# A hybrid diffusion backbone on one core: two conditioning groups move from VectorE reductions to TensorE matmuls

## The chip, the core and the metric

The kernel runs on one core of a Trainium2 chip. TensorE (PE) multiplies, VectorE (DVE), ScalarE (ACT) and GpSimd (POOL) do everything else, and SyncE (SP) issues most of the DMAs. Each engine runs its own list of instructions strictly in order and waits where an operand is not there yet. The metric is the device time of one execution in microseconds. The kernel before has a median of 2817.92 us over three runs (2812.58 to 2819.59).

## What is computed

The program is two layers over 1024 latent tokens and 256 context tokens of width 1024. The first layer mixes with a Fourier transform and a long convolution, the second with attention. What matters here is the conditioning. Each layer turns the two conditioning vectors `c` and `c_ctx` into six groups of 1024 modulation values each:

```python
def ada_mod(cond, w, b):
    m = (jax.nn.silu(cond) @ w + b)[..., None, :]
    return jnp.split(m, 6, axis=-1)

sh1, sc1, g1, sh2, sc2, g2 = ada_mod(c, ada_w[i], ada_b[i])
u_lat = modulate(rms_norm(h_lat, norm1_g[i]), sh1, sc1)
...
h_lat = h_lat + g1 * y_lat
h_lat = h_lat + g2 * swiglu(modulate(rms_norm(h_lat, norm2_g[i]), sh2, sc2), ...)
```

The first two groups of layer 0 (`sh1`, `sc1`) are needed at the very start. The third and fourth (`g1`, the gate behind the mixer, and `sh2`, the shift ahead of the feed-forward part) are needed only when the output projection of the mixer is evicted, several hundred microseconds later. All of it is 32-bit arithmetic.

## The kernel before, in words

Activations lie with channels on the 128 partitions. A modulation value is therefore a column: `self.ada[(layer, c)]` is a tile of 128 x 48, and column `nb` holds outputs 128·nb to 128·nb+127. A group is eight such columns, and two groups are sixteen blocks of 128 outputs.

The program is written as Python generators that are stepped in turn. `in_proj` (L1091) walks over sixteen blocks of the input projection. For each block it loads one 128 x 1024 slice of `w_in`, splits it into a high and a low part on ACT and DVE, and multiplies. Between the matmuls of a block it steps filler generators: the filters of the long convolution (`long` and `filt`), the small Fourier part, and `ada`. The table of numbers at its call (L2833 and L2834) says how many steps of each filler belong to which block; `ada` begins with the sixth block. A planner then sets the final order on each engine from its own estimate of when things are ready, so that the lists of PE, DVE, ACT, POOL and SP that run on the chip are fixed before the run.

`ada_first` (L501) makes the first two groups on TensorE. The two vectors stand as 2 columns, the weights move past them 512 outputs at a time, and the 2 x 512 result is a row. Tiny matmuls of 2 x 128 against an identity (L348, from the helper `mm`) turn the row into columns, and DVE adds the bias.

`late_groups((2, 3), "ws")` (L621) makes the third and fourth group on VectorE. `load_cond` (L539) brings `c` and `c_ctx` to all 128 partitions and applies Silu on ACT. `ada_group` (L550) loads one 512 KB block of `ada_w` ahead of its use, into a tile of the ring `ws`, which has four buffers and also serves the loads of `w_in`. `ada_block` (L572) then makes four multiply-and-sum reductions over 512 elements (L580): two halves for each of the two vectors. The lines that follow use these names: L580 is the reduction, L333 the DMA from SP's queue, L844 the product of a filter with its window, L352 and L354 the high and the low part of a split, L1085 to L1088 the short convolution.

Of the kernel before, what the change touches and what calls it, by code (L numbers as in the profile page):

```python
# [16 lines left out]
MUL, ADD, SUB, MAX, MIN = ALU.mult, ALU.add, ALU.subtract, ALU.max, ALU.min  # L17

P = 128
D = 1024  # L20
KB = D // P
# [14 lines left out]
def _f32(a):  # L36
    return np.ascontiguousarray(a, dtype=np.float32)
# [221 lines left out]
class Builder:  # L259
# [241 lines left out]
    def ada_first(self):  # L501

        nc, a = self.nc, self.a
        cond = self.C(16)
        self.ld(cond, a["cond"])
        nc.scalar.activation(cond, cond, AF.Silu)
        yield

        def columns(m, ps):
            col = self.PS()  # L510
            for j in (0, 1):
                row = self.G()
                nc.vector.tensor_copy(row[0:2, :], ps[j][0:2, :])
                for k in range(4):
                    nb = 4 * j + k
                    with self.follow(last):
                        self.mm(col[:, 2 * nb:2 * nb + 2], row[0:2, k * P:(k + 1) * P], self.ident[0:2, 0:2], True, True)
            sl = slice(m * 8, m * 8 + 8)
            for c in (0, 1):
                t = self.ada[(0, c)]  # L520
                nc.vector.tensor_tensor(t[:, sl], col[:, 0:16].rearrange("p (n c) -> p c n", c=2)[:, c],
                                        self.adab[:, sl], ADD)
                if m == 1:
                    nc.vector.scalar_tensor_tensor(t[:, sl], t[:, sl], 1.0, self.gs[:, 0:8], op0=ADD, op1=MUL)

        ps = {}
        for m in (1, 0):
            ps[m] = [self.PP(), self.PP()]
            for kb in range(KB):
                w = self.W("ws", "ws") if m == 0 and kb > KB - 3 else self.S4()  # L530
                self.ldr(w, a["ada_k"][m, kb])
                for j in (0, 1):
                    last = nc.tensor.matmul(ps[m][j][0:2, :], cond[:, 2 * kb:2 * kb + 2], w[:, j * 512:(j + 1) * 512],
                                            start=kb == 0, stop=kb == KB - 1).ins
                yield
        for m in (1, 0):
            columns(m, ps[m])
# [55 lines left out]
    def ada_stream(self, groups, n):  # L593

        blocks = [(l, m, m * 8 + k, conds) for l, m, conds in groups for k in range(8)]

        def step(b, st):
            l, m, nb, conds = b
            self.ada_block(l, nb, [st[:, :512], st[:, 512:]], conds)
            if nb % 8 == 7:  # L600
                self.ada_done(l, m, conds)

        own = [self.S4() for _ in range(3)]
        for k in range(0, n, 3):
            with self.follow(self.last_hi):
                for t, b in zip(own, blocks[k:k + 3]):
                    self.lda(t, self.a["ada_w"][b[0], b[2]])
            yield
            with self.follow(self.last_lo):
                for t, b in zip(own, blocks[k:k + 3]):  # L610
                    step(b, t)
            yield
        for k, b in enumerate(blocks[n:]):
            t = own[k % 3]
            with self.follow(self.last_ldr):
                self.ldr(t, self.a["ada_w"][b[0], b[2]])
            with self.follow(self.last_lo):
                step(b, t)
            yield

    def late_groups(self, ms, where):  # L621

        self.load_cond(wide=where == "s4")
        for m in ms:
            yield from self.ada_group(0, m, (0, 1), where)
# [2144 lines left out]
    def run(self):  # L2770
        nc, a = self.nc, self.a
# [27 lines left out]
        def filters():  # L2799
            gens = [self.filter_raw("l", raws["l"], (o,)) for o in (0, 1)]  # L2800
            next(gens[0])
            yield
            for o in (0, 1):
                tot = self.filter_sum("l", o, raws["l"][o])
                for k, _ in enumerate(gens[o]):
                    if k > 1 and k % 2 == 0:
                        next(tot)
                    yield
                for k, _ in enumerate(self.spectrum_l(o, raws["l"][o], tot)):
                    if o == 0 and k == 5:  # L2810
                        next(gens[1])
                    yield

        long = filters()
        ada = self.late_groups((2, 3), "ws")
        filt = (x for o in (0, 1) for g in (self.filter_raw("c", raws["c"], (o,)), self.spectrum_c(o, raws["c"][o]))
                for x in g)
        self.Y = {}
# [2 lines left out]
        def four():  # L2821
            y.t.update(self.new_act(pcs=(2,), blocks=range(4)).t)
            yield from self.fourier_c(y)

        def conv():
# [5 lines left out]

        fc, cc = four(), conv()
        self.in_proj(u, ng, ((long, (1, 2, 4, 5, 5, 5, 5, 5, 6, 0)), (filt, (0,) * 9 + (3, 3, 3, 3, 2)),  # L2833
                             (ada, (0,) * 5 + (1, 1, 2, 1, 2, 1, 2, 1, 2, 1, 2))), fc, cc)  # L2834
        self.held = False
        for i in range(8):
            self.tap(f"u{i}", u.ap(0, i, 0))
# [120 lines left out]
        h2, o, h4 = Act(), Act(), Act()  # L2958
# [62 lines left out]
        for i, _ in enumerate(first_part(1)):  # L3021
            if i == 7:
                c = self.rms_begin(0)
# [53 lines left out]
        c = self.rms_begin(1)  # L3077
# [11 lines left out]
def host_layout(i):  # L3089
    f = {k: np.asarray(v) for k, v in i.items()}  # L3090
    o = {}
    o["x_t"] = f["x"][0].T.reshape(KB, P, LAT)
    o["ctx_t"] = f["ctx"][0].T.reshape(4, 2, P, CTX).transpose(0, 2, 1, 3).reshape(4, P, 512)
    o["x_row"] = np.concatenate([f["x"][0], f["ctx"][0]]).reshape(10, P, D)
    o["c"] = f["c"].reshape(1, D)
    o["c_ctx"] = f["c_ctx"].reshape(1, D)
    o["ada_k"] = f["ada_w"][0, :, :2 * D].reshape(KB, P, 2, D).transpose(2, 0, 1, 3)
    o["cond"] = np.stack([f["c"].reshape(KB, P), f["c_ctx"].reshape(KB, P)], axis=1).transpose(2, 0, 1).reshape(P, 16)
    o["ada_w"] = f["ada_w"].transpose(0, 2, 1).reshape(2, 48, P, D)
    o["ada_b"] = f["ada_b"].reshape(96, P).T  # L3100
    gs = np.concatenate([f["norm1_g"].reshape(16, P), f["norm2_g"].reshape(16, P), f["final_g"].reshape(8, P)])
    o["gs"] = gs.T

    def wblk(w):
        k, n = w.shape
        return w.reshape(k // P, P, n // P, P).transpose(2, 1, 0, 3).reshape(n // P, P, k)

    o["w_in"] = wblk(f["ab_w_in"][0])
    o["w_out"] = wblk(f["ab_w_out"][0])
    o["w_out2"] = wblk(f["na_w_out"][0])  # L3110
    o["gate"] = np.stack([wblk(f["ffn_w_gate"][l]) for l in range(2)])
    o["up"] = np.stack([wblk(f["ffn_w_up"][l]) for l in range(2)])
    o["down"] = f["ffn_w_down"].reshape(2, NFB, P, 2, 512).transpose(0, 1, 3, 2, 4)
    qkv = f["na_w_qkv"][0]
    o["wq"] = wblk(qkv[:, :D])
    o["wk"] = wblk(qkv[:, D:2 * D])
    o["wv"] = qkv[:, 2 * D:].reshape(4, 2, P, 2, 512).transpose(3, 0, 2, 1, 4).reshape(2, 4, P, 1024)
    w1, w2 = f["hy_f_w1"][0], f["hy_f_w2"][0]
    z1 = np.zeros((66, P), np.float32)
    z1[:33, :64], z1[33:, 64:] = w1, w1  # L3120
    z2 = np.zeros((P, P), np.float32)
    z2[:64, :64], z2[64:, 64:] = w2, w2
    o["w1f"], o["w2f"] = z1, z2
    o["mlpv"] = np.stack([np.tile(f[k][0], 2) for k in ("hy_f_b1", "hy_f_b2", "hy_f_freq")], axis=1)
    o["w3"] = np.concatenate([f["hy_f_w3"][0]] * 2, axis=0)
    cw = np.concatenate([f["hy_conv_w"][0], f["hy_conv_b"]], axis=0)
    o["conv"] = cw.reshape(4, 12, P).transpose(2, 0, 1).reshape(P, 48)
    o["skip"] = f["hy_bias"][0].reshape(8, P).T
    o["skiprow"] = f["hy_bias"][0].reshape(2, HC)
    rpb = f["na_rpb"][0]  # L3130
    bias = np.full((16, 2, 4, P, 384), NEG, np.float32)
    for hf in range(2):
        for r in range(8):
            row = 8 * hf + r
            rs = min(max(row - 4, 0), 8)
            for c in range(4):
                for w in range(16):
                    qc = 16 * c + w
                    ws = min(max(qc - 8, 0), 48)
                    for kr in range(rs, rs + 8):  # L3140
                        c0 = (kr - 4 * hf) * 32 + ws - KSTART[c]
                        dc = ws - qc + 15
                        bias[:, hf, c, r * 16 + w, c0:c0 + 16] = rpb[:, kr - row + 7, dc:dc + 16]
    o["bias"] = bias
    return {k: _f32(v) for k, v in o.items()}
# [20 lines left out]
```

## Time and profile before

| | |
|---|---|
| median of three runs | 2817.92 us (2812.58 to 2819.59) |
| the profiled execution's own time | 2812.72 us |
| its span, first to last instruction | 2810.8 us |
| PE busy | 2695.3 us, 96% of the span |
| DVE busy | 2129.7 us, 76% |
| ACT busy | 1631.0 us, 58% |
| mean granted TensorE clock | 0.986 |
| sixteen blocks of the two groups: loads issued | from 104.4 us to 433.7 us |
| their reductions on DVE | from 240.2 us to about 457 us |

The columns of the views are these. A row of the stretches gives the busy time of PE, PE's weight load, DVE, ACT and POOL with the number of instructions in brackets, then the granted TensorE clock as a share of full speed, the DMA share and the rate in GB/s. A row of the groups gives line, engine, operation, output and inputs by tile name, shapes and count, and after the bar the busy time, the mean length of one in ns, and the idle time of the engine just before with what ended it. A row of the waits gives who waited, for whom, the total in us, the number of times and the longest. A row of the timeline gives the start in us, the length in us, and in square brackets the idle time ahead of it with what ended it. Matmuls are pipelined: the length of one is longer than the distance to the next, so a price per matmul is read from start to start.

### The profile page before, as it was taken

The numbers are of one execution on the slowest core, as the hardware profiler recorded it, in microseconds if no ns is written. First come the engines' busy times: TensorE is split into PE (matmuls) and PEld (weight loads), VectorE is DVE, ScalarE is ACT, GpSimd is POOL, SyncE is SP. The second block draws the span as 40 slices with busy tenths as digits, with TensorE's granted clock in tenths as the row PEclk, the third lists the DMA queues.
The fourth block names the chain that finished last, engine by engine and source line by source line (L and its number), as shares of the span: only waits on it lengthen the run. The fifth ranks groups of instructions, "written<-read, shape, count | busy, mean of one in ns | idle before, by whom it ended". The sixth has DMA issues, their size and how long they took to land. (4 is left out here: it accounts for less than half of the span.)

```text
span 2810.8 us, 44489 instructions
## 1 busy us (share of the span) xinstructions
PE 2695.3 (96%) x15570; PEld 1717.7 (61%) x15570; DVE 2129.7 (76%) x3870; ACT 1631.0 (58%) x3005; POOL 514.1 (18%) x820
## 2 busy tenths in 40 slices
PE   6999889999999999999999999999989999999998
PEld 3877677878889444444446646767677544444445
DVE  4678788868776899987798646878786877775775
ACT  3533324543487666767556736888774655654653
POOL 2120233351101011122011002333222012221000
PEclk9999899999999999999999999999999999999999
DMA  7244736766655787787988746788955246654863
GB/s 267 95 148 164 226 93 196 232 197 226 213 168 173 244 292 287 284 314 276 360 308 287 238 153 161 193 202 199 253 180 192 89 140 222 224 191 168 296 224 105
DMA packets 312317, 595.92 MB, mean 212 GB/s; under 512 B 83352, under 2 KB 130138, under 8 KB 312094
## 3 DMA queue, kind: packets, MB, share of 16 engines
q1 hardware_dynamic: 241374, 378.61, 42.6%
q0 software_dynamic: 53760, 158.38, 16.3%
q10 hardware_dynamic: 16960, 56.11, 5.8%
q8 instruction: 122, 2.00, 0.3%
q14 instruction: 101, 0.83, 0.1%
HBM read 445.64 MB, written 119.80 MB: 201 GB/s over the span
## 5 line engine op out<-in xcount | busy, mean ns | idle before, releaser
L2080 PE MATMUL ps<-s,s 128*128 128x512 f16 x2280 | 508.9, 379 | 5.6 <-DVE s L2104 3.1
L2080 PEld LDWEIGHTS <-s 128*128 128x128 f16 x2640 | 258.0, 98 | 320.5 <-issue 10.1
L348 PE MATMUL ps<-s,wh 128*128 128x256 f32 (+1 forms) x1784 | 413.8, 334 | 9.3 <-ACT wh L352 6.1
L348 PEld LDWEIGHTS ps<-s,wh 128*128 128x128 f32 x1784 | 300.3, 191 | 44.6 <-ACT wh L352 8.0
L2344 PE MATMUL ps<-s 128*128 128x512 f16 (+2 forms) x1404 | 316.1, 376 | 0.2 <-ACT s L2334 0.2
L2344 PEld LDWEIGHTS <-s 128*128 128x128 f16 x1716 | 166.1, 98 | 196.1 <-issue 5.3
L348 PE MATMUL ps<-s,wl 128*128 128x256 f32 (+1 forms) x892 | 273.0, 332 | 3.2 <-DVE wl L354 3.2
L2334 ACT ACTIVATE s<-s,c 128x512 f16<-128x512 f32 (+1 forms) x300 | 199.9, 714 | 118.7 <-DMA s<-d 63.0
L348 PE MATMUL ps<-s,s 128*128 128x65 f16 (+4 forms) x2748 | 242.4, 238 | 19.3 <-DMA s<-tk 5.0
L2335 DVE SCALAR_TENSOR_TENSOR s<-s,c,s 128x512 f16<-128x512 f32 (+1 forms) x300 | 208.6, 747 | 33.2 <-ACT s L2334 32.7
L339 POOL DMA_DIRECT2D d<-s x245 | 132.9, 544 | 503.6 <-DVE s L2197 170.5
L2080 PE MATMUL ps<-s,hl 128*128 128x512 f16 x924 | 212.2, 379 | 1.2 <-ACT hl L1933 1.2
L348 PE MATMUL pq<-s,hl 128*128 128x512 f16 (+1 forms) x960 | 206.9, 358 | 0.4 <-DVE s L2587 0.4
L348 PEld LDWEIGHTS ps<-s,wl 128*128 128x128 f32 x892 | 168.2, 192 | 21.9 <-DVE wl L354 4.9
L2080 PEld LDWEIGHTS <-hl 128*128 128x128 f16 x1056 | 103.2, 98 | 125.9 <-ACT hl L1933 1.4
L1933 ACT ACTIVATE hl<-ws,c 128x1024 f16<-128x1024 f32 x89 | 101.8, 1144 | 107.8 <-DMA ws<-in_up 37.7
L1934 DVE SCALAR_TENSOR_TENSOR hl<-ws,c,hl 128x1024 f16<-128x1024 f32 x89 | 114.0, 1283 | 62.6 <-ACT hl L1933 62.3
L348 PEld LDWEIGHTS <-s 128*128 128x128 f16 x2400 | 115.2, 98 | 66.8 <-DMA s<-tk 5.7
L348 PEld LDWEIGHTS ps<-s,s 128*128 128x128 f32 (+1 forms) x828 | 128.6, 191 | 35.7 <-PE ps L348 9.5
L1934 DVE SCALAR_TENSOR_TENSOR s<-t,c,s 128x512 f16<-128x512 f32 x176 | 126.6, 747 | 26.3 <-ACT s L1933 26.3
L348 PEld LDWEIGHTS <-hl 128*128 128x128 f16 x960 | 86.8, 98 | 80.3 <-issue 8.8
L1933 ACT ACTIVATE s<-t,c 128x512 f16<-128x512 f32 x176 | 118.1, 714 | 9.2 <-DVE t L2059 5.6
(541 smaller groups left out, 5115.9 us busy)
## 6 DMA issues: line engine op xcount, KB each, us to landing
s<-d SPq DMA_DIRECT2D x326, 256.0 KB, 4.9
d<-s POOLq DMA_DIRECT2D x229, 256.0 KB, 4.5
s<-in_down SPq DMA_DIRECT2D x150, 256.0 KB, 6.4
ws<-in_gate SPq DMA_DIRECT2D x42, 512.0 KB, 4.7
ws<-in_up SPq DMA_DIRECT2D x42, 512.0 KB, 6.0
s<-in_ada_w POOLq DMA_DIRECT2D x34, 512.0 KB, 6.5
d<-s SPq DMA_DIRECT2D x60, 256.0 KB, 2.5
s<-in_ada_w ACTq DMA_DIRECT2D x30, 512.0 KB, 7.4
```

What stands on the lines that cost most here:

```text
L339: self.last_ldr = self.nc.gpsimd.dma_start(out, in_).ins
L348: self.last_mm = self.nc.tensor.matmul(o, l, r, start=st, stop=sp).ins
L1933: self.last_hi = self.nc.scalar.activation(hi, src, AF.Copy, scale=s).ins
L1934: self.last_lo = self.nc.vector.scalar_tensor_tensor(lo, src, s, hi, op0=MUL, op1=SUB).ins
L2080: nc.tensor.matmul(ps, x[:, sl], y, start=first and j == 0 and x is wh and y is xh, stop=j == 3 and x is wl, skip_group_check=True)
L2334: self.last_hi = nc.scalar.activation(x, f[:, c:c + 512], AF.Copy, scale=s).ins
L2335: self.last_lo = nc.vector.scalar_tensor_tensor(y, f[:, c:c + 512], s, self.raw_part(x), op0=MUL, op1=SUB).ins
L2344: m = nc.tensor.matmul(acc[j][:, c0:c1], x[:, sl], y[:, xs], start=first and k == 0, stop=last and k == 2, skip_group_check=True)
```

## The change

The third and fourth group go to TensorE. Sixteen slices of the weights are laid out on the host as blocks of 128 outputs, with the 1024 inputs as eight slabs of 128 (`ada_c`). For each block, eight matmuls of 128 moving columns run against the two conditioning columns that `ada_first` already made (`condc`), and their sum is a row pair of 2 x 128 in a PSUM tile of the `ps` ring. DVE copies the 2 x 128 row pair into the front of the block's own weight tile. One step of the generator later, a tiny matmul against the identity turns the pair into two columns in the same PSUM tile, and two DVE additions of 128 x 1 put them into `self.ada` with the bias. The broadcast loads of `c` and `c_ctx` for these groups and their Silu go away. The load stays 512 KB a block, one block ahead, in the same ring, but a tile of the ring is now free after the turn rather than after the last reduction. The last entries of the step table go from `1, 2` to `2, 2`, since the last turn needs one more step. The later groups keep their reductions on DVE.

```diff
-        cond = self.C(16)
+        cond = self.condc = self.C(16)
...
+    def column_groups(self, ms):
+
+        nc, a = self.nc, self.a
+        blocks = [m * 8 + k for m in ms for k in range(8)]
+        ready = []
+
+        def load(nb):
+            t = self.W("ws", "ws")
+            self.ld(t, a["ada_c"][nb - 16])
+            ready.append(t)
+
+        load(blocks[0])
+        for k, nb in enumerate(blocks):
+            if k + 1 < len(blocks):
+                load(blocks[k + 1])
+            w = ready.pop(0)
+            ps = self.PP()
+            for kb in range(KB):
+                self.mm(ps[0:2, 0:P], self.condc[:, 2 * kb:2 * kb + 2], w[:, kb * P:kb * P + P], kb == 0, kb == KB - 1)
+            nc.vector.tensor_copy(w[0:2, 0:P], ps[0:2, 0:P])
+            yield
+            self.mm(ps[:, P:P + 2], w[0:2, 0:P], self.ident[0:2, 0:2], True, True)
+            for c in (0, 1):
+                nc.vector.tensor_tensor(self.ada[(0, c)][:, nb:nb + 1], ps[:, P + c:P + c + 1], self.adab[:, nb:nb + 1],
+                                        ADD)
...
-        ada = self.late_groups((2, 3), "ws")
+        ada = self.column_groups((2, 3))
...
-                             (ada, (0,) * 5 + (1, 1, 2, 1, 2, 1, 2, 1, 2, 1, 2))), fc, cc)
+                             (ada, (0,) * 5 + (1, 1, 2, 1, 2, 1, 2, 1, 2, 2, 2))), fc, cc)
...
+    o["ada_c"] = f["ada_w"][0, :, 2 * D:4 * D].reshape(KB, P, 16, P).transpose(2, 1, 0, 3).reshape(16, P, D)
```

The first place is on PE, in the filters of the context tokens inside the input projection. `s_48` holds their hidden values, `g` a scaled filter weight, `pq` and `ps` are PSUM tiles. Before:

```order
L348 MATMUL pq_3016<-g_2994,s_48_172 128x512
L348 MATMUL pq_3070<-s_783_2882,s_798_2912 128x256
L348 MATMUL pq_3070<-s_783_2882,s_799_2913 128x256
L348 MATMUL pq_3070<-s_783_2882,s_798_2912 128x256
L348 MATMUL ps_3082<-s_783_2882,s_798_2912 128x256
L348 MATMUL ps_3082<-s_783_2882,s_799_2913 128x256
L348 MATMUL ps_3082<-s_783_2882,s_798_2912 128x256
L348 MATMUL ps_3011<-g_2989,s_48_172 128x512
L348 MATMUL pq_3016<-g_2995,s_48_172 128x512
```

With the change:

```order
L348 MATMUL ps_3045<-ws_2876,c_102 2x128 x8
L348 MATMUL ps_3021<-g_2999,s_48_172 128x512
L348 MATMUL ps_3069<-ws_3043,c_102 2x128
L348 MATMUL pq_3026<-g_3004,s_48_172 128x512
L348 MATMUL ps_3069<-ws_3043,c_102 2x128 x3
L348 MATMUL pq_3026<-g_3005,s_48_172 128x512
L348 MATMUL ps_3069<-ws_3043,c_102 2x128 x4
L348 MATMUL pq_3090<-s_764_2892,s_779_2922 128x256
L348 MATMUL pq_3090<-s_764_2892,s_780_2923 128x256
L348 MATMUL pq_3090<-s_764_2892,s_779_2922 128x256
L348 MATMUL ps_3045<-c_86,ws_2876 128x2
```

Two blocks' matmuls (`ws` is the weight block, `c_102` the two vectors) now stand among the filter's, and the turn of the first of them (`c_86` is the identity) comes three matmuls after the second block's last one.

The second place is DVE's list around the same filter products. L844 in the kernel before is L870 in the changed one, and L640 and L644 are the copy and the additions of the change. Before:

```order
L580 ISA t_3054,c_98<-ws_3030,s_559_2066,ah_3051 128x512
L580 ISA c_98 128x1
L580 ISA ws_3030,ah_3056<-ws_3030,s_556_2059,c_101 128x512
L580 ISA ah_3056 128x1
L844 TENSOR_TENSOR s_820_3014<-ps_3011,s_817_2998 128x512
L844 TENSOR_TENSOR s_822_3019<-pq_3016,s_817_2998 128x512
```

With the change:

```order
L354 TENSOR_TENSOR g_3005<-t_3002,g_3004 128x512
L640 COPY ws_2876<-ps_3045 2x128
L870 TENSOR_TENSOR s_801_3024<-ps_3021,s_798_3008 128x512
L870 TENSOR_TENSOR s_803_3029<-pq_3026,s_798_3008 128x512
L640 COPY ws_3043<-ps_3069 2x128
L644 TENSOR_TENSOR c_97<-ps_3045,c_101 128x1
L644 TENSOR_TENSOR c_98<-ps_3045,c_101 128x1
```

The reductions ahead of the filter products are gone, and one copy of 2 x 128 stands there. The second copy stands behind both products.

## The prediction

> **What bounds the kernel now.** I read the page first, then stretches of time around the change, then who waits there, then the instructions that the change removes or resembles. The page says that TensorE is busy nearly all the time and that the chain that ended last is made of its matmuls.
>
> ```profile
> span 2810.8 us, 44489 instructions
> PE 2695.3 (96%) x15570; PEld 1717.7 (61%) x15570; DVE 2129.7 (76%) x3870; ACT 1631.0 (58%) x3005; POOL 514.1 (18%) x820
> PE 23%; DVE 2%; ACT 1%; issue 0%; DMA 0%; DVEq 0%; POOL 0%; ACTq 0%
> ```
>
> So time saved on DVE counts only where PE stands still, and every microsecond added to PE counts unless it lands in a hole. The average hides where the holes are; the stretches show it.
>
> ```profile
> core 0: us, PE busy (x) PEld busy (x) DVE busy (x) ACT busy (x) POOL busy (x), PEclk, DMA share, GB/s
> 80.00:160.00 80.00, 79.54 (x435) 68.00 (x434) 55.55 (x108) 36.66 (x71) 16.67 (x22) 1.00 0.33 107
> 160.00:190.00 30.00, 29.21 (x141) 21.82 (x141) 22.27 (x47) 10.94 (x22) 6.45 (x12) 0.94 0.54 167
> 190.00:460.00 270.00, 239.50 (x1134) 190.55 (x1133) 223.81 (x487) 94.06 (x172) 52.22 (x71) 0.93 0.52 162
> 340.00:350.00 10.00, 7.90 (x31) 7.05 (x32) 9.74 (x35) 2.61 (x9) 0.49 (x1) 0.50 0.61 191
> ```
>
> From 190 to 460 us, the rest of the input projection, PE idles 270 - 239.5 = 30.5 us. Its granted clock is 0.93 there, so 7% of the cycles are missing; over the 239.5 busy us that is 16.8 us of work done slowly. At full clock and without holes this stretch holds 239.5 - 16.8 = 222.7 us of PE work, and 47.3 us are slack. DVE is at 223.8 of 270, 83%. In 340 to 350 DVE is full (9.74 of 10), PE has holes, and the clock is at half. From 80 to 160, with DVE at 55.55 of 80 (69%), PE is full at clock 1.00.
>
> The waits of PE in that stretch:
>
> ```profile
> PE ps L348 <- ACT s L352: 10.3, 6, 3.8
> PE ps L348 <- ACT g L352: 6.3, 3, 2.9
> PE ps L348 <- DVE s L354: 3.6, 3, 2.2
> PE ps L348 <- DMA tk<-in_ff_l: 2.2, 1, 2.2
> PE ps L348 <- DVE s L1633: 1.9, 1, 1.9
> PE ps L348 <- DVE s L844: 1.8, 1, 1.8
> ```
>
> These are operands that ACT and DVE split. One of them shows how the conditioning takes part:
>
> ```profile
> 342.82 0.74 DVE L580 CUSTOM_DVE_ANT_0 ws<-ws,s,ah 128x512 f32<-128x512 f32 x1
> 343.49 0.74 DVE L580 CUSTOM_DVE_ANT_0 t<-ws,s,ah 128x512 f32<-128x512 f32 x1
> 344.16 0.74 DVE L580 CUSTOM_DVE_ANT_0 ws<-ws,s,c 128x512 f32<-128x512 f32 x1
> 345.44 0.68 DVE L844 TENSOR_TENSOR s<-pq,s 128x512 f32<-128x512 f32 x1
> 345.57 0.80 PE L348 MATMUL ps<-s,wh 128*128 128x256 f32 x2 [1.82 <-DVE s L844]
> ```
>
> Three reductions stand ahead of a filter product on DVE, and PE waits 1.82 us for it.
>
> **What goes.** The reductions and their accumulator reads:
>
> ```profile
> L580 DVE CUSTOM_DVE_ANT_0 t<-ws,s,c 128x512 f32<-128x512 f32 x16 | 13.3, 831 | 0.4 <-ACT s L547 0.4
> L580 DVE CUSTOM_DVE_ANT_0 ws<-ws,s,ah 128x512 f32<-128x512 f32 x16 | 12.5, 780 | 0.0
> L580 DVE CUSTOM_DVE_ANT_0 ws<-ws,s,c 128x512 f32<-128x512 f32 x16 | 12.3, 770 | 0.0
> L580 DVE CUSTOM_DVE_ANT_0 t<-ws,s,ah 128x512 f32<-128x512 f32 x16 | 12.3, 769 | 0.0
> 190.00:460.00 270.00, 48.99 (x128) 0.93 0.52 162
> ```
>
> The last row is the same stretch for L580 alone: 49.0 us of DVE time (the four groups sum to 50.4, since neighbours overlap a little at their ends). Four Silu on ACT and four broadcast loads on SP go too; a table load on ACT moves to the next group's Silu. I cost these at nothing either way, as ACT is busy only 94.1 of 270. If that cover were gone they would be worth a little, all on the gaining side.
>
> **What comes on PE.** 128 matmuls of 128 moving columns and 16 turns. A 32-bit matmul of this kind is recorded as two instructions: the first two groups have 16 x 2 matmuls of 512 columns and 64 records. So 256 and 32 instructions come. Their nearest rows, with the start of what follows each:
>
> ```profile
> 39.56 13.04 PE L533 MATMUL ps<-s,c 128*2 128x512 f32 x30
> 52.43 3.60 PE L533 MATMUL ps<-ws,c 128*2 128x512 f32 x8
> 58.31 1.94 PE L348 MATMUL pq<-c,g 2*128 2x2 f32 x16
> 60.18 0.44 PE L740 MATMUL pq<-c,s 128*128 128x128 f32 x2
> 466.00 1.97 PE L1299 MATMUL ps<-c,s 128*128 128x128 f32 x8 [4.43 <-DVE s L354]
> ```
>
> 512 columns take (52.43 - 39.56)/30 = 0.429 us from start to start, a quarter of that is 0.107. The tiny turns take (60.18 - 58.31)/16 = 0.117, though they move only two columns. No row has 2 stationary and 128 moving columns. The low end is 0.107; the high end is the 0.246 of the last row (1.97/8), 128 columns right after a hole. I take 0.117, because it is measured in dense work and the scaled price lies just below it: 256 x 0.117 = 30.0 and 32 x 0.117 = 3.7, together 33.7 us (31.1 to 66.7).
>
> The Trainium skill, TensorE: Matmul & The Clock Gate, section Back-to-back issue gap, gives about 81 ns for each pair of weight load and matmul at 128 columns in a sustained stream, and FP8 and Floating Point Precision, section TensorE Precision Notes, gives four passes to a true 32-bit matmul. By these an estimate would be 128 x 4 x 0.081 = 41.5 us in place of 30.0. The measured 0.429 us for two passes of 512 speaks for the lower price, and no row here has the case itself.
>
> **What comes on DVE.** Sixteen copies of 2 x 128 and 32 additions of 128 x 1, both out of PSUM:
>
> ```profile
> L513 DVE COPY g<-ps 2x512 f32<-2x512 f32 x4 | 2.7, 679 | 15.4 <-PE ps L533 15.4
> 163.17 0.16 DVE L885 COPY c<-ps 128x4 f32<-128x4 f32 x1
> L1087 DVE SCALAR_TENSOR_TENSOR s<-ps,c,s 128x1 f32<-128x1 f32 x10 | 2.1, 208 | 0.0
> ```
>
> Between 0.16 us for 4 and 0.68 for 512 elements, 128 come to 0.16 + 0.52 x 124/508 = 0.29 us. That is 16 x 0.29 + 32 x 0.208 = 11.3 us. DVE falls to 223.8 - 49.0 + 11.3 = 186.1 us, 69% of 270, the share that it has from 80 to 160.
>
> **The sum.** PE then holds 222.7 + 33.7 = 256.4 us at full clock in a stretch that now takes 270. What is left of the slack decides. From 80 to 160 PE works at 99.4% of its full rate (79.54/80), from 160 to 190 at 91.5% (29.21 x 0.94/30), with DVE at 74%. Neither range has reductions. The stretch in question has filters and spectra like the second and a DVE share like the first, so I take the middle, 95%: 256.4/0.95 = 269.9, no change. The bounds are 256.4/0.994 = 257.9 (-12) and 256.4/0.915 = 280.2 (+10).
>
> The change adds one wait: a turn on PE waits for its copy on DVE, and behind it in PE's list stand the projection's own matmuls, whose results DVE and ACT want next. At the place shown, the turn is three matmuls behind the last of the second block, and its copy has one split ahead of it. Nothing, if the copy has run by then, to some 0.7 us if it stands behind one more 128 x 512 instruction (0.68 us, L844 above); I take 0.25 on average, 16 x 0.25 = +4. The ring brings a wait on the other side: SP waited for the reductions to free its buffers, and the stores behind it waited too.
>
> ```profile
> SPq L333 <- DVE c L580: 37.0, 9, 18.8
> ws<-in_ada_w SPq DMA_DIRECT2D x16, 512.0 KB, 3.7
> ```
>
> Now the turn frees them. A block lands in 3.7 us and is issued a step ahead, sixteen steps in 270 us, so I cost the loads at nothing; if that cover went, each late block would hold PE for up to 3.7 us. Other orders behind 460 us shift by a few instructions; I take zero, a few microseconds both ways.
>
> So the profiled execution of 2812.7 us (span 2810.8 and 1.9 around it) would become 2816.7. The median of the runs lies 5.2 above that execution; carried to it, the forecast is 2817.9 + 4 = 2822 us, a change within 0.3% (8.4 us, about what a measurement of this kernel tells from none).
>
> **The rivals.** First, faster: DVE's relief closes the holes as from 80 to 160, and the filling keeps the clock up. For it, DVE's share becomes the same, and the half clock at 340 to 350 sits beside full DVE. Against it, ACT's splits and one DMA are named in the waits too, and the holes from 160 to 190 come without any reduction. It gives -12, with the turns hidden: 2806 us.
>
> Second, slower: the turns become PE's new wait. PE cannot pass a turn whose copy is behind DVE work, sixteen times. In full stretches a copy stands behind two or three instructions of 0.68 to 0.8 us; at 1.2 us a turn this costs 16 x 1.2 = 19 in place of 4, so 2837 us. Its point: above 0.53 us a turn, 8.4/16, the change is slower by more than 0.3%. For it, DVE is still 69% busy and its list is strict; against it, the planner spread most turns several matmuls behind the copies. The same side is reached if PE only gets the 91.5% of 160 to 190.
>
> Third, slower by the price of the matmuls: the weight load does not hide behind 128 columns as it does behind 512.
>
> ```profile
> L533 PEld LDWEIGHTS ps<-s,c 128*2 128x2 f32 x56 | 4.8, 88 | 30.5 <-issue 17.4 <-DMA s<-in_ada_k 13.0
> ```
>
> Each then costs 0.107 + 0.088 = 0.195 us: 256 x 0.195 + 3.7 = 53.6 us, so (222.7 + 53.6)/0.95 = 290.8, and with the turns +25: 2843 us. Against it, the turns keep 0.117 with a load each. The 81 ns of the skill would come out between, at (222.7 + 41.5 + 3.7)/0.95 = 282 and +16 with the turns.
>
> **How the numbers follow.** The forecast, within 0.3%, has 0.42. Faster has 0.25. The second rival has 0.27 and the third 0.06, together 0.33 for slower. The forecast's own range is 2809 to 2826. The range for 8 in 10 takes in the first rival with a few microseconds below and the second with a few above: 2802 to 2840.
>
> **What would show it.** Right: from 190 to about 465 us PE is above 93% busy at a clock of 0.96 or more, DVE falls to about 69%, the new matmuls stand 0.11 to 0.12 us apart, and PE's waits for the copy sum to under 8 us. The first rival would show the projection ending 10 us earlier. The second would show PE waiting for the copies as its first row of waits. The third would show the new matmuls near 0.2 us apart with PE busy. I would be wrong altogether if the time moved behind 460 us, where only the order of a few loads and matmuls differs.

## The result, and the profile after

The kernel with the change takes 2834.3 us (median of four runs, 2833.45 to 2836.54). The kernel before, on the same chip, takes 2815.9 us (2812.58 to 2819.59). The ratio is 1.0059, with a 95% interval of 1.0044 to 1.0074: slower by 0.6%, 18.4 us. That lies inside the range of 2802 to 2840, but in the case to which the prediction gave 0.33, not in its likeliest.

The page of the profile after, first three parts (busy time, share of the span, instructions; then the chain that ended last, by engine):

```profile
span 2832.0 us, 44960 instructions
PE 2731.8 (96%) x15858; PEld 1737.9 (61%) x15858; DVE 2094.0 (74%) x3790; ACT 1627.5 (57%) x3001; POOL 513.2 (18%) x820
PE 21%; DVE 2%; issue 1%; ACT 0%; DMA 0%; POOL 0%; DVEq 0%; POOLq 0%; ACTq 0%
```

The span grew by 21.2 us, PE's busy time by 36.5, and DVE's fell by 35.7. PE has 288 instructions more, as counted beforehand. To place the loss, take the moment at which the input projection's last piece begins on PE: 449.5 us before and 465.7 us after. The stretch from 190 us to that moment, in each kernel (length, then busy time of PE, weight load, DVE, ACT and POOL, then the granted clock, DMA share and GB/s). Before:

```profile
190.00:449.50 259.50, 230.79 (x1088) 182.97 (x1087) 213.38 (x453) 86.93 (x160) 51.34 (x70) 0.94 0.51 161
449.50:2810.80 2361.30, 2297.20 (x13675) 1414.92 (x13673) 1794.78 (x3185) 1465.31 (x2702) 425.44 (x685) 0.99 0.68 221
```

After:

```profile
190.00:465.70 275.70, 261.06 (x1347) 200.09 (x1346) 179.22 (x380) 83.33 (x155) 50.71 (x71) 0.97 0.48 151
465.70:2832.00 2366.30, 2303.24 (x13704) 1418.01 (x13702) 1793.35 (x3177) 1465.62 (x2702) 424.86 (x683) 0.99 0.67 220
```

16.2 us are lost in the projection, and 5.0 behind it. The second part differs between the kernels of this study by more than that (2354 to 2368 us in their profiled executions, with nearly the same work in it), so only the first part is explained here. In that part PE's idle time did fall, from 28.7 to 14.6 us, the clock rose from 0.94 to 0.97, and DVE has room. Multiplied out, PE delivers 261.06 x 0.97 / 275.7 = 91.9% of its full rate, against 230.79 x 0.94 / 259.5 = 83.6% before. The holes were filled, but not enough of them for the work that came.

The new instructions in the groups of the profile after (window 190 to 480 us):

```profile
L348 PE MATMUL ps<-ws,c 128*2 128x128 f32 x256 | 35.1, 296 | 0.9 <-ACT t L884 0.9
L348 PE MATMUL ps<-c,ws 2*128 2x2 f32 x32 | 6.1, 256 | 0.0
```

They are busy for 41.2 us. No row of PE's waits names a copy. PE's waits, SP's queue and DVE in the same stretch (who waited for whom, us in total, times, longest):

```profile
PE ps L348 <- ACT s L352: 7.6, 2, 3.8
PE pq L348 <- ACT s L352: 2.6, 1, 2.6
...
SPq L333 <- PE ps L348: 54.5, 17, 10.4
...
DVE ws L640 <- PE ps L348: 13.3, 7, 4.2
DVE c L644 <- PE ps L348: 8.4, 7, 3.9
```

So PE waits for ACT in three places for 10.2 us. SP's queue, which waited 37.0 us for the reductions before, now waits 54.5 us for PE. (That sum alone is no sign of the loss: in two kernels below that are not slower, e8 and e4, it is 75.0 and 77.5 us.) DVE stands 13.3 us in front of the copies and 8.4 us in front of the sums.

### The profile page after: what moved, and what is told of

Same layout as the page of the kernel before. It is cut to its first block, busy times and chain, and to the rows that moved or that the text cites. A ratio compares the mean times of both kernels' runs of the same rounds, so it can differ in the third digit from the quotient of the medians.

```text
span 2832.0 us, 44960 instructions
## 1 busy us (share of the span) xinstructions
PE 2731.8 (96%) x15858; PEld 1737.9 (61%) x15858; DVE 2094.0 (74%) x3790; ACT 1627.5 (57%) x3001; POOL 513.2 (18%) x820
```

## The experiments

All ratios below are to the kernel before on the same chip. "The end of the projection" is the moment defined above, from the profiled execution. The recorded texts number their theories per set of runs; here they go by what they claim.

Two limits hold for the ends. Each comes from one execution, while the kernel before alone spreads from 2810.74 to 2830.87 us over the 35 executions beside the last four kernels; a difference of a few us between two ends says little by itself. And the kernels differ a little ahead of the stretch: the same split of weights on ACT begins at 193.1 us in the kernel before and in the change, at 198.5 in e1, 196.5 in e4, 196.3 in e2, 196.0 in e6, 194.5 in e3b and e7, and within 0.6 us of 193.1 in the others. Where this matters, the difference counted from that split is given too.

**Which half of the change costs: four corners.** The first kernel leaves both products away and keeps the loads; the second keeps DVE's reductions beside the new products.

```diff
 e1_neither: column_groups
-            for kb in range(KB):
-                self.mm(ps[0:2, 0:P], ...)
-            nc.vector.tensor_copy(w[0:2, 0:P], ps[0:2, 0:P])
             yield
-            self.mm(ps[:, P:P + 2], w[0:2, 0:P], ...)
             # the sums read w[:, c:c + 1]
 e2_both: column_groups
+        self.load_cond(wide=False)
...
+                    nc.vector.tensor_tensor_reduce(self.T(), w[:, j * 512:j * 512 + 512], self.cond[c][j], ...)
             nc.vector.tensor_copy(w[0:2, 0:P], ps[0:2, 0:P])
```

> Leaves out the products of the third and fourth group: neither the 128 matmuls and 16 turns on TensorE nor the reductions on VectorE; the loads and the bias additions stay, so those two groups hold a wrong value. Absorbing theory: the holes of TensorE between 190 and 450 us are made by chains that the reductions hardly lengthen, and the change only fills them with its own matmuls. Then taking both away returns little: 2808 to 2818 us, TensorE's idle time between 190 us and the end of the projection stays at 20 us or more. Relief theory: the holes were made by the reductions ahead of other work on VectorE, and the 20 us of slack that the change returned came from that. Then this kernel is about 20 us below before, 2794 to 2799 us, and the idle time falls to about 15 us.

> The changed kernel with the four reductions of each block kept on VectorE as well (on the same tile, their sums into columns that are overwritten later). Absorbing theory: the holes are filled by the matmuls all the same, so it is about as the changed kernel, 2834 to 2840 us. Relief theory: without relief the matmuls cost their full 37 us, 2848 to 2855 us.

Without either product: 2807.1 us, ratio 0.9964 (0.9954 to 0.9975), projection's end at 440.8. With both: 2843.1 us, 1.0098 (1.0078 to 1.0117), end at 478.4. Before to neither, and both to the change, DVE's relief is worth 0.4%; neither to the change, and before to both, TensorE's side costs 0.95 to 0.98%, some 27 us. The two add up, and TensorE's side costs two thirds of its 41 busy us. Both times lie between the two theories of the recorded texts. That looked like a dear filling of the holes; the later runs showed that it is not.

**Half of the blocks, either half.** The third group on PE and the fourth on DVE, then the other way round.

```diff
 e3_half:  column_groups((2,)), then late_groups((3,), "ws")
 e3b_half: late_groups((2,), "ws"), then column_groups((3,))
```

> The third group on TensorE as in the change, the fourth on VectorE as before: half of the added matmul work, some 19 us, and half of the relief. Absorbing theory: the 20 us of slack that the change could fill take this work whole, so 2814 to 2820 us, no change against before. Proportional theory (each block costs the same): half of the loss, about 2825 us.

> The other half: the third group on VectorE as before, the fourth on TensorE. Additive theory (27 us for the matmuls of sixteen blocks, 10 us back from the reductions of sixteen): +8.5 against before. If the loss belongs to the blocks of the third group, whose half run came out at +15: 0 to +3. If half the work costs as much as all of it: +15.

2832.1 us, ratio 1.0055 (1.0035 to 1.0074), end 463.3; and 2827.1 us, 1.0024 (1.0005 to 1.0043), end 464.1. Half of the new PE work, and the projection ends only about 2 us earlier than with all of it (2 to 3 counted from the split). By that end the cost does not go by PE's work; by the ratios the first half costs as much as the whole, and the second less than half of it.

The second also shows that the turns are not all. Its first new matmul begins at 396.1 us, and by then it has already lost 6.6 us on the kernel before: the 128x256 matmuls of the seventh block of the projection begin at 211.0 us against 209.6, those of the thirteenth at 385.4 against 377.4. The planner orders all lists anew for every kernel, and what another order costs by itself was not separated from the rest.

**The table alone.** The kernel before, with only the step table's last `1, 2` turned into `2, 2`.

```diff
-                             (ada, (0,) * 5 + (1, 1, 2, 1, 2, 1, 2, 1, 2, 1, 2))), fc, cc)
+                             (ada, (0,) * 5 + (1, 1, 2, 1, 2, 1, 2, 1, 2, 2, 2))), fc, cc)
```

> The kernel before with only the step table of the change. It moves a handful of instructions near the end of the projection. Theory that the matmuls make the loss: within 3 us of before. Rival theory that the loss is made by the planner's other order and not by the matmuls: 5 to 15 us slower.

2812.1 us, ratio 0.9977 (0.9959 to 0.9995), end 449.2. The table by itself is not the loss. This one reordering came out 0.2% faster; how far the planner's other orders move the kernel it does not tell.

**The products in another shape.** First the operands swapped: the weights stand, and the two vectors move, so that the result is a column and no turn is needed. Then products in one 16-bit pass, with the weights rounded by ACT, and the turns kept.

```diff
 e6_wstat
-                self.mm(ps[0:2, 0:P], self.condc[:, 2 * kb:2 * kb + 2], w[:, kb * P:kb * P + P], ...)
-            nc.vector.tensor_copy(w[0:2, 0:P], ps[0:2, 0:P])
+                self.mm(ps[:, 0:2], w[:, kb * P:kb * P + P], self.condc[:, 2 * kb:2 * kb + 2], ...)
             yield
-            self.mm(ps[:, P:P + 2], w[0:2, 0:P], ...)
 e7_f16
+            w16 = self.T(F16, 1024)
+            nc.scalar.copy(w16, w)
-                self.mm(ps[0:2, 0:P], self.condc[:, 2 * kb:2 * kb + 2], w[:, ...], ...)
+                self.mm(ps[0:2, 0:P], cond16[:, 2 * kb:2 * kb + 2], w16[:, ...], ...)
```

> The changed kernel with the operands of its matmuls swapped: the weight block of 128 x 128 stands still and the two vectors move, so the sums come out as columns; no turn, no copy to the weight tile. The nearest row, 128 x 1 moving against a 32-bit block of 128 x 128, gives 0.115 us an instruction, the price of the change's own matmuls, so what goes are the 32 instructions of the turns, 6 us of TensorE: 2827 to 2830 us. If the turns lay in holes: 2834 us, as the change. If the weight load of 128 columns (0.19 us) is not hidden: 256 x 0.07 = 18 us more, 2845 us or above.

> The changed kernel with the weight blocks copied to 16-bit tiles on ScalarE and the two vectors in 16 bits, so that each matmul is one pass (lower precision, 16 copies of some 1.1 us more on ScalarE). TensorE work falls from 41 us to about 128 x 0.06 + 6 = 14 us. Theory that the TensorE work makes the loss at 0.7 of its length: 19 us below the changed kernel, about 0 against before. Rival theory that the number of matmuls, the turns or the waits around them count and not their length: +10 or more.

Swapped: 2822.0 us, ratio 1.0013 (0.9995 to 1.0030), end 462.6. That is less than any of the three cases of the recorded text. It has no turn and ends its projection nearly as late as the kernels with turns, but in its own way, which the last section shows: its clock there is 0.92. The 16-bit products: 2827.9 us, 1.0030 (1.0011 to 1.0049), end 462.6, although the matmuls are down from 35.1 to 10.6 us of PE:

```profile
L348 PE MATMUL ps<-t,c 128*2 128x128 f16 x128 | 10.6, 237 | 3.4 <-ACT t L640 3.4
```

24.5 us less of PE's work brought the projection's end forward by 3.1 us (4.5 counted from the split). The work alone does not decide. The test is not a pure one, though: the rounding puts 16 more casts of about 1.05 us each on ACT, for which PE waits in turn, and by the ratio about half of the change's loss is gone.

**Without turns and copies.** All 128 products stay; the turns and copies go.

```diff
 e4_noturn
-            nc.vector.tensor_copy(w[0:2, 0:P], ps[0:2, 0:P])
             yield
-            self.mm(ps[:, P:P + 2], w[0:2, 0:P], self.ident[0:2, 0:2], True, True)
             # the sums read w[:, c:c + 1]
```

> The changed kernel without turns and copies; the 128 matmuls stay, and the additions read two columns of the weight tile, so the two groups hold wrong values. Theory from the two-by-two runs: TensorE work counts at about 0.7 of its length (27 us for 39), the turns are 6 us of it, so 4 to 5 us below the changed kernel, +12 to +14 against before. Rival theory that the turns cost much more than their own time, because what follows them on TensorE waits for the copy: 10 us or more below the changed kernel, +7 or less.

2816.9 us, ratio 0.9985 (0.9967 to 1.0004), end 452.4: 13.3 us earlier than the change, for 6.1 us of turns. The stretch:

```profile
190.00:452.40 262.40, 252.07 (x1334) 196.85 (x1333) 179.50 (x369) 83.92 (x157) 52.20 (x72) 0.99 0.53 165
```

The products of fifteen of the sixteen blocks are in it, as in the change's stretch, and the projection ends 11.6 us later than with none at all (440.8; 13.6 counted from the split). Most of the rest of the change's loss is something about the turns or the copies.

**Which of the two, and can it be had without.** Three kernels split them. One keeps the copies, but no turns. One keeps the turns, but reads them from the loaded tile, so that nothing on PE waits for DVE. One keeps both, with each dependent piece a step later, the rows in tiles of their own, and the eight turns of a group together; a fourth adds the 16-bit products to it.

```diff
 e9_copy
             nc.vector.tensor_copy(w[0:2, 0:P], ps[0:2, 0:P])
             yield
-            self.mm(ps[:, P:P + 2], w[0:2, 0:P], self.ident[0:2, 0:2], True, True)
             # the sums read w[:, c:c + 1]
 e10_turn
-            nc.vector.tensor_copy(w[0:2, 0:P], ps[0:2, 0:P])
             yield
             self.mm(ps[:, P:P + 2], w[0:2, 0:P], self.ident[0:2, 0:2], True, True)
             # the sums read w[:, c:c + 1]
 e8_batch
+            rows[k // 4] = self.S2()                       # every fourth block
+            nc.vector.tensor_copy(rows[k // 4][0:2, k % 4 * P:k % 4 * P + P], done[k][0:2, 0:P])   # a step later
...
+            for k in range(8):                             # once a group
+                self.mm(cols[g][:, 2 * k:2 * k + 2], rows[2 * g + k // 4][0:2, k % 4 * P:k % 4 * P + P], ...)
 e11_f16batch: e8_batch with the products of e7_f16
```

> The change with the same 256 new matmul instructions and 32 turning ones, but each dependent piece one step later: a block's two rows are copied in the step after their matmuls, into two free 128x512 tiles, the eight turns of a group follow together, and the sums (two of 128x8 a group instead of sixteen of 128x1) one step behind them. PE's work stays, and DVE's copies and sums find their data ready. Theory A (in the change DVE, which runs in order, is held at the copies for 13.3 us and at the sums for 8.4 us until PE has done the products and turns, and what stands behind on DVE comes late to PE): DVE waits under 4 us at the new lines, the input projection ends near 453 us instead of 465.7, ratio to before 0.998 to 1.001 (2810 to 2818 us). Theory B (the price is PE's own work on products and turns, 41 us, whatever the order): projection's end 462 to 466 us, ratio 1.004 to 1.007 (2827 to 2837 us).

> The change without its 32 turning instructions, but with the copies behind the matmuls kept (leaves out: the turns; the sums take columns of the copied tile, so the modulation values of groups three and four are not the reference's). Theory A: DVE still waits 13 us or so at the copies, so about 60% of the 20 us between the change and the kernel without turns and copies stays: ratio 1.001 to 1.004 (2818 to 2827 us), projection's end 457 to 462 us. Theory C (the turns on PE cost it, by standing in PE's order behind a wait): as without both, ratio 0.997 to 1.000 (2807 to 2815 us), end near 452 us. Theory B: 6 us of turns less than the change, ratio 1.003 to 1.005.

> The change with its turns, but without the copies: the turns take the first two rows of the loaded weight tile, and the sums read that tile (leaves out: copy and use of the turned columns, so the modulation values of groups three and four are not the reference's). PE has all its 288 new instructions, DVE nothing that waits for PE. Theory A: close to the kernel without turns and copies, plus the turns' 6 us of PE at about half their length: ratio 0.998 to 1.001 (2810 to 2818 us), projection's end 452 to 456 us. Theories B and C: nearly the change, ratio 1.003 to 1.006 (2824 to 2833 us), end 460 to 466 us.

> The kernel with turns in groups of eight and later copies, and in addition one-pass 16-bit products (weight blocks rounded to 16 bits by ACT): 128 instructions of some 11 us instead of 256 of 35 us. Theory A: both costs are gone, ratio 0.993 to 0.998 (2796 to 2810 us), faster than the kernel before and than the change, and close to the kernel without any product (0.9964). Theory B: PE's new work is down from 41 to 17 us, which by the earlier 16-bit run (1.003) gives 1.001 to 1.004 again (2818 to 2827 us).

| kernel | median, us | ratio to before | projection's end |
|---|---|---|---|
| copies, no turns (e9) | 2813.3 | 0.9974 (0.9958 to 0.9990) | 447.8 |
| turns, no copies (e10) | 2832.3 | 1.0043 (1.0028 to 1.0057) | 465.9 |
| later copies, turns in eights (e8) | 2815.0 | 0.9982 (0.9967 to 0.9997) | 450.6 |
| the same with 16-bit products (e11) | 2815.6 | 0.9983 (0.9968 to 0.9998) | 447.4 |

The theory that DVE is held in front of the copies, on which I had put most before these runs, falls, although e8 came out as it had forecast. With the copies kept, DVE waits at them as long as in the change (15.0 us over all sixteen in both; the 13.3 us above leave out the last block), and the kernel is fast. Waits and stretch of the kernel with copies alone:

```profile
DVE ws L640 <- PE ps L348: 15.0, 8, 4.6
...
190.00:447.80 257.80, 247.79 (x1316) 193.88 (x1315) 179.47 (x381) 83.31 (x155) 50.84 (x71) 0.99 0.53 166
```

The turns alone, with no wait of PE for DVE or of DVE for PE at the new lines, bring the loss back (ratio 1.0043 against 1.0059, the same projection's end):

```profile
190.00:465.90 275.90, 260.15 (x1349) 201.08 (x1348) 176.15 (x365) 83.19 (x155) 51.40 (x71) 0.96 0.50 153
```

And the turns in eights, the same 32 instructions, do not:

```profile
190.00:450.60 260.60, 251.02 (x1336) 197.16 (x1336) 177.05 (x354) 83.33 (x155) 51.01 (x71) 0.98 0.51 161
L348 PE MATMUL ps<-c,s 2*128 2x2 f32 x32 | 4.2, 249 | 0.0
```

**What a lone turn does.** A lone turn is one that is made a block at a time, not in eights. The ring `ws` has four tiles, for the conditioning blocks and for the projection's own weights, `in_w_in`. In the change a block's rows lie in its weight tile, so the tile is given back by the turn, one step of the generator after the last product. Put the turns on PE beside SP's weight loads. PE in the change, a block's products and two of the turns:

```profile
253.98 1.91 PE L348 MATMUL ps<-ws,c 128*2 128x128 f32 x16 [0.90 <-ACT t L884]
267.50 0.38 PE L348 MATMUL ps<-c,ws 2*128 2x2 f32 x2
...
374.88 0.38 PE L348 MATMUL ps<-c,ws 2*128 2x2 f32 x2
```

SP's queue in the change:

```profile
267.91 0.33 SPq L333 DMA_DIRECT2D ws<-in_w_in  x1
...
375.29 0.33 SPq L333 DMA_DIRECT2D ws<-in_w_in  x1
```

Both loads are issued 0.41 us after a turn begins. That holds for six of the seven weight loads that are issued once the turns have begun (0.40 to 0.41 us each); the seventh comes 1.5 us after one. The kernel with turns in eights, the same block, then the same weight load:

```profile
253.88 1.91 PE L348 MATMUL ps<-ws,c 128*2 128x128 f32 x16 [0.90 <-ACT t L906]
...
255.82 0.33 SPq L333 DMA_DIRECT2D ws<-in_w_in  x1
```

The products stand at the same time in both, 253.9 us. Here the load goes out as they end, at 255.82, and in the change at 267.91: 12.1 us later. The kernel with turns alone shows the change's picture (turn, then load):

```profile
376.27 0.38 PE L348 MATMUL ps<-c,ws 2*128 2x2 f32 x2
...
376.68 0.33 SPq L333 DMA_DIRECT2D ws<-in_w_in  x1
```

The split of the weights on ACT follows the load. The third split of the stretch starts at 271.4 us in the change, and at 270.9, 277.8, 276.3, 270.9 and 268.1 in the other five with lone turns (e10, e7, e2, e3, and e3b, which still holds its tile for a reduction at that point). It starts at 259.4 to 263.2 in the five that free it early (e4, e6, e8, e9, e11), and at 266.4 in the kernel before, whose reductions hold it. The seventh, in the change and in the kernel with copies alone:

```profile
379.25 1.05 ACT L352 CAST wh<-ws 128x1024 fp32r<-128x1024 f32 x1 [2.17 <-DMA ws<-in_w_in]
```

```profile
364.39 1.05 ACT L352 CAST wh<-ws 128x1024 fp32r<-128x1024 f32 x1 [0.93 <-DMA ws<-in_w_in]
```

14.9 us apart, when PE in the two kernels was only some 6.6 us apart. In the change the turn that frees this tile comes 7.0 us after its block's last product; the planner has set the load behind two stores on SP, so that SP itself stands only 0.4 us before this turn. PE is in no hurry for these weights: it first uses them at 404.0 us, and at 387.8 us with copies alone. DVE is. It makes the low half of the split, and behind that, in DVE's list, stands the chain that ends in the operand PE waits for next. The low half on DVE, in the change and with copies alone:

```profile
380.66 1.21 DVE L354 TENSOR_TENSOR wl<-ws,wh 128x1024 fp32r<-128x1024 f32 x1
```

```profile
365.47 1.23 DVE L354 TENSOR_TENSOR wl<-ws,wh 128x1024 fp32r<-128x1024 f32 x1 [4.72 <-ACT wh L352]
```

From there DVE is busy nearly all the time (11.74 of 11.78 and 13.56 of 13.77 us) until the chain's copy out of PSUM, at 392.44 and 379.24 us: 13.2 us apart, twice PE's distance. The projection's matmuls are what covers PE while this chain runs. In the change all 72 of the block in hand are done by 389.65, before the chain's result is there; PE's timeline with two idle gaps, then the stretch between two conditioning blocks' products, the one behind it, and the time around the second gap (columns as above):

```profile
364.30 0.39 PE L348 MATMUL pq<-s,c 128*2 128x512 f32 x1 [2.64 <-ACT s L352]
389.37 0.28 PE L348 MATMUL ps<-s,wl 128*128 128x256 f32 x1
393.44 2.37 PE L348 MATMUL ps<-s,tk 128*128 128x512 f32 x4 [3.79 <-ACT s L352]
...
364.85:395.74 30.89, 27.10 (x139) 20.70 (x139) 17.98 (x41) 7.41 (x18) 6.97 (x9) 0.90 0.24 73
395.74:420.82 25.08, 25.07 (x138) 19.38 (x137) 13.84 (x42) 6.78 (x17) 8.29 (x9) 0.92 0.46 142
393.00:400.00 7.00, 6.56 (x25) 3.60 (x26) 2.09 (x8) 1.98 (x4) 0.57 (x1) 0.53 0.29 94
```

The same two stretches with copies alone, where the last of the same block's 72 matmuls still run until 380.8 us and the chain's result is there:

```profile
358.27:381.88 23.61, 23.61 (x138) 19.13 (x138) 17.67 (x41) 7.18 (x18) 6.86 (x8) 1.00 0.30 91
381.88:404.46 22.58, 22.02 (x131) 17.76 (x130) 14.84 (x42) 6.71 (x16) 8.35 (x9) 1.00 0.54 163
```

7.3 and 2.5 us, 9.8 of the 17.9 by which the two projections differ: 3.8 us of idling, and then half clock for about 7 us, as the 0.53 shows. The idle gap of 2.64 us before 364.3 was followed by another 3.4 us at half clock. The rest is spread in pieces of 1 to 4 us, part of it the 6.1 us of turns. The kernel with turns alone has the same picture at this place: load at 376.68, low half at 381.88, copy out of PSUM at 393.80, and idle gaps of 1.51 and 2.25 us at 390.8 to 395.1. The Trainium skill, TensorE: Matmul & The Clock Gate, says in its section Why this matters for your kernels that PE should have no idle gap over about 3 us between bursts. The trace agrees as to the gap of 3.79 us, and shows that 2.64 us can be enough.

One kernel that would close the argument was not run: the change with lone turns where they are, and only the rows put into another tile. Shown are the 0.41 us between turn and load, the late splits, one place at which a late split becomes idle time, and that every kernel with lone turns is late and every kernel that frees the tile early has its weights early. That the turn hurts by nothing but the tile it holds is argued from these. The planner's order is the rival that stays: it also sets where the loads and the matmuls stand, and it cost e3b 6.6 us with no new matmul in the way.

## Why the prediction came out as it did

The time came to lie inside the stated range, but that is luck as far as the mechanism goes: the likeliest case, a change within 0.3%, did not come, and nothing in the range was worked out for late weights.

- **The price of the new matmuls** held. A dense block takes 0.115 us an instruction (1.91 us for 16 with the last one's tail, from 232.76 to 234.60), against 0.117 taken. Busy time is 41.2 instead of 33.7, since busy times count the overlapping tail and since some blocks ran at half clock (16 instructions from 364.85 took 3.05 us). The third rival, an unhidden weight load at 0.195, did not come.
- **The 95% rate** held where the weights were early and all the 32-bit products of 128 moving columns stood on PE. The kernel without turns and copies reaches 252.07 x 0.99 / 262.4 = 95.1%, the one with copies alone 95.2% and, with turns in eights, 94.4%. It is no rate of the stretch as such: with no product it is 88.5%, with the swapped operands 88.8%, with 16-bit products and turns in eights 87.8%. The prediction's sum, that 33.7 us more of PE work would leave the projection as long as it was, is what e8 shows: 260.6 against 259.5 us.
- **The step that failed** is the costing of the ring: "Now the turn frees them. A block lands in 3.7 us and is issued a step ahead, sixteen steps in 270 us, so I cost the loads at nothing". It looked at the conditioning blocks alone, which indeed have time. It left out that the projection's weights take their tiles from the same four, and that a lone turn, placed many matmuls behind, gives its tile back late: the turns begin 1.6 to 14.1 us after their block's last product, and one weight load went out 12.1 us later than in e8. The text ahead of the prediction states both facts, the shared ring and the release by the turn. Its price is the difference between the change and e8, 1.0059 against 0.9982, 0.77% or some 22 us in the ratios and 15.1 us in the projection. That the held tile makes all of it is argued, as said above; that the lone turns make it is what e9, e10 and e8 show.
- **The second rival** had the time, 2837 us, and the place, the turn. Its mechanism was wrong. PE does not wait at the turns: no row of its waits names a copy, and the turns cost the same when no copy exists (e10). The further a turn stands behind its products in PE's list, the longer it holds its tile; by this account, what I counted against the rival is what made the loss.
- **The first rival's** mechanism is there too. Without the reductions and with nothing new on PE, PE's idle time falls from 28.7 to 19.6 us, the clock rises from 0.94 to 0.96 and the kernel is 0.36% faster (e1). Filling the holes then keeps the clock up: with the products and copies alone PE idles 10.0 us at 0.99, and 28.8 us of products cost 7.0 us of projection (440.8 to 447.8; 13.0 counted from the split). In the change this gain is outweighed.
- **The signs that were to show it right** all came: PE at 94.7%, a clock of 0.97, DVE at 65%, matmuls 0.115 us apart, no wait for copies. They were too weak. 93% at 0.96 is 89% of the full rate, well under the 95% on which the sum stood, and none of them looked at when the weights arrive.

## What to carry to other kernels

When a change moves the release of a buffer, ask for every user of its ring, not only for the data of the change: the one that waits may be another stream on another queue, and the engine that idles shows a third name in its waits (here PE's waits name ACT). A small dependent step that is put far behind its producer so that nobody waits for it holds whatever it reads for that long; give its input a small tile of its own. Here e8, which does that, copies a step later and gathers the turns, makes of a change that is slower by 0.6% one that is faster by 0.2% (0.9982, 0.9967 to 0.9997); the small tile by itself was not run.

## What was not expected of the hardware

TensorE went into half clock while it was busy, within a burst of matmuls that move only two columns. In the kernel with swapped operands, the group of such matmuls, one burst, an earlier burst's stretch (290.4 us), the stretches before and behind the first one's start, and the whole:

```profile
L348 PE MATMUL ps<-c,ws 128*128 128x2 f32 x256 | 34.4, 264 | 0.0
433.67 4.79 PE L348 MATMUL ps<-c,ws 128*128 128x2 f32 x32
290.40:297.00 6.60, 6.60 (x49) 6.17 (x49) 5.27 (x12) 3.65 (x6) 0.88 (x2) 1.00 0.75 217
428.00:435.00 7.00, 7.00 (x41) 6.04 (x39) 6.93 (x15) 3.55 (x6) 1.16 (x2) 1.00 0.68 219
435.00:442.00 7.00, 7.00 (x34) 6.61 (x34) 2.19 (x9) 0.27 (x1) 2.24 (x2) 0.56 0.47 150
190.00:462.60 272.60, 263.10 (x1332) 219.06 (x1331) 180.69 (x372) 84.41 (x157) 50.59 (x71) 0.92 0.51 158
```

PE is busy 7.00 of 7 us on both sides, and yet the clock falls from 1.00 to 0.56 within the burst. Over the whole stretch PE is 96.5% busy at 0.92. It does not happen each time: of the twelve bursts six are followed by half clock, two of them with no idle time just ahead (433.7 and 468.0 us), and the other six are not, the one of 32 instructions at 290.4 us among them. What decides was not found. In the change, the products of 128 moving columns did this nowhere in the projection without an idle gap ahead of them.

Also, taking work from a PE that is well filled need not help. With 16-bit products the projection of e11 has 13 us less of PE's work than e8, and is 3.2 us shorter:

```profile
190.00:447.40 257.40, 237.96 (x1201) 189.15 (x1200) 178.08 (x353) 99.35 (x172) 49.88 (x71) 0.95 0.53 165
```

The clock falls from 0.98 to 0.95 and the idle time rises from 9.6 to 19.4 us, and the two kernels' ratios are the same within their intervals.
